# First product of an MLP's second stage made inside the last block of its first stage, and late weight differences queued behind factor splits

## The chip, the cores and the metric

The kernel runs on one core of one Trainium2 chip. A core has five engines with a queue of instructions each: TensorE (PE: matmuls, with PEld for its weight loads), VectorE (DVE), ScalarE (ACT), GpSimd (POOL) and SyncE (SP, which here only issues transfers). Each engine takes its instructions in the order that was fixed when the program was built; engines wait for one another through semaphores. The metric is the device time of one execution in microseconds; the figure of a kernel is the median over runs.

## The reference

One layer of a hybrid encoder: an input projection, a state-space mixer and a neighbourhood attention, an output projection, and an MLP. Only the last line matters here; the rest is left out. All arrays are float32, with 1024 tokens, `D_MODEL` = 1024 and `D_FF` = 4096.

```python
...
    x = x + jnp.concatenate([y_ssm, y_na.astype(y_ssm.dtype)], axis=-1) @ w_out
    h = rmsnorm(x, norm_mlp_w)
    return x + jnp.square(jax.nn.relu(h @ w_mlp_in)) @ w_mlp_out
```

## The kernel before

**Precision.** PE multiplies float32 operands that were rounded to a shorter form (`F32R`). So every operand is split: its high part is a copy by ACT into that form (line 761), its low part the rest, src - high, by DVE or POOL (line 762). `chain` (line 745) makes one matrix product of three matmuls: high x high, high x low, low x high. Weights are split with POOL for the low part, activations ("factors") with DVE.

**Both MLP stages** use a scheme of Strassen's kind: a product of two 2 x 2 block matrices takes seven block products instead of eight, in the order `ORD` = 1, 2, 6, 5, 7, 3, 4, over sums and differences of the blocks. Products 1, 6, 7 and 4 are summed in one set of PSUM banks (`X`), 2 in a second and 5 and 3 in a third (`Y`).

**Stage one** (lines 1124 to 1272) makes relu(h @ w_mlp_in)^2 in eight blocks of 512 columns (`Block`, fb = 0 to 7). A product is 24 matmuls of 128 x 128 by 512. Its factors `hc[1]` to `hc[7]` stay in SBUF for all blocks; the tiles of products 1 to 3 are tags `h10` to `h31` of pool `hA`. A block's weights come in four tiles ("11", "12", "21", "22", `raw_tile`, eight in a ring, two in pool `wp` and six in `wq`); `split` makes the high and low tile of a product's weights through `w_split` (line 1119), whose ring `hls` has three pairs `wh`/`wl`, all in `wp`. `X` is two of the four PSUM banks `mm` (`ps_mm`, line 107), so that two blocks' sums can be live at once. `sums` brings the results to SBUF, squares them, forms the factors of stage two, and `store` writes these to `act_dr`. In the last block the stores are issued by POOL, else by SP.

**Stage two** (lines 1275 to 1377) multiplies with `w_mlp_out` in four blocks of 1024 rows (fb = 0 to 3). A product is 48 matmuls: for each of four token tiles t, two halves u of the rows, two quarters a, and the three of `chain`. `a_load` reads a factor from `act_dr` (pool `ar`, four tiles), `a_split` splits it (`ahl`: pools `a1`, `a2`, `a3` with two pairs each), weights are loaded into `raw_of` tiles and split through `w_split`, now with `hls` = three pairs in `wy` and three in `wp`. Line 1373 adds each result to `acc`, which was loaded from `x2_dr` (line 1355). Before product 6 DVE forms the weight differences `t1` and `t2` (lines 1343 and 1344), before product 7 that of line 1346, before product 4 that of line 1348.

**Places.** Pools are placed over one another: the tiles of stage two lie where stage one's lay, and each waits for the last use of the tile below it. By sizes and sides, `ar` lies over `h10` and `h11`, `a1` over `h20` and `h21`, `a2` over `h30` and `h31`, `ra` (weights "21") and `x0` (the first half of `acc`) over the tiles of products 7 and 4, `rb` (weights "12" and "22") over the factors of 6 and 5, `wy` over `wq`, and `x1` and `a3` over the tiles `cq` of `sums`. PSUM pool `ps3` of stage one is closed at its end, and `ps4` takes its banks.

**Order.** Nobody writes out the queues. At build a scheduler runs the traced program through a model of the machine and puts next on each engine, among the instructions that are ready there, the one traced first. A tile of a pool with several buffers is given a buffer when one is free. `tc.issue_after(i)` keeps what is traced within it behind instruction i on the same engine, without a wait.

## Time and profile before

| what | value |
|---|---|
| median of 3 runs | 1672.34 us (1671.72 to 1681.54) |
| the profiled execution, its own time | 1682.42 us |
| its span in the trace | 1680.6 us |
| granted TensorE clock, mean | 0.984 |
| DVE, ACT, POOL busy in the span | 1031.1, 722.1, 727.7 us |
| HBM read, written | 189.40 MB, 86.56 MB |
| last block of stage one, from its product 1 | from about 1318.3 us of the span |
| stage two, from its first matmul | from 1361.15 us to the end |

The profile's views used here are: the page (busy time of each engine), rows of busy time by stretch (start and end in microseconds of the span, length, busy time and count for each engine, granted TensorE clock, share of the DMA engines and GB/s), rows of instructions in order of time (start, length, engine, line, operation, output<-inputs, shape, count, and in brackets the idle time of the engine before it with what ended it), and the chain of waits (start, length, engine, output, line). Names are those of the program without buffer numbers: `px`, `py`, `pz` are PSUM banks, `wh` and `wl` weights' high and low parts, `h` stage one's factors, `ahl` stage two's, `wraw` weights as loaded, `cq` stage one's results. A matmul's end is modelled and overlaps the next one's start. Line 747 is the matmul in `chain` for both stages: `px<-h,wh` is stage one, `px<-wh,ahl` stage two.

### The profile page before, as it was taken

The numbers are of one execution on the slowest core, as the hardware profiler recorded it, in microseconds if no ns is written. First come the engines' busy times: TensorE is split into PE (matmuls) and PEld (weight loads), VectorE is DVE, ScalarE is ACT, GpSimd is POOL, SyncE is SP. The second block draws the span as 40 slices with busy tenths as digits, with TensorE's granted clock in tenths as the row PEclk, the third lists the DMA queues.
The fourth block names the chain that finished last, engine by engine and source line by source line (L and its number), as shares of the span: only waits on it lengthen the run. The fifth ranks groups of instructions, "written<-read, shape, count | busy, mean of one in ns | idle before, by whom it ended". The sixth has DMA issues, their size and how long they took to land. (4 is left out here: it accounts for less than half of the span.)

```text
span 1680.6 us, 20886 instructions
## 1 busy us (share of the span) xinstructions
PE 1596.8 (95%) x7461; PEld 1301.1 (77%) x7461; DVE 1031.1 (61%) x1438; ACT 722.1 (43%) x1195; POOL 727.7 (43%) x522
## 2 busy tenths in 40 slices
PE   6999999999988889999999989999999979999999
PEld 5788888777776678887887867788888868888887
DVE  5776314788886853566675567444343387887863
ACT  5434223334343432566566533544444544433330
POOL 4000003877787861233335233344444464455551
PEclk9999999999999999999999999999999999999999
DMA  8213336866675885978565241353344386644231
GB/s 207 61 38 104 90 99 195 218 195 186 226 231 176 221 256 192 275 201 221 167 183 169 89 150 51 113 178 136 138 163 151 114 294 243 213 151 150 100 101 75
DMA packets 180290, 274.01 MB, mean 163 GB/s; under 512 B 14603, under 2 KB 105819, under 8 KB 180187
## 3 DMA queue, kind: packets, MB, share of 16 engines
q1 hardware_dynamic: 136203, 231.77, 45.1%
q10 hardware_dynamic: 42976, 37.23, 7.3%
q0 software_dynamic: 1008, 3.67, 0.5%
q8 instruction: 59, 0.97, 0.2%
q14 instruction: 44, 0.36, 0.1%
HBM read 189.40 MB, written 86.56 MB: 164 GB/s over the span
## 5 line engine op out<-in xcount | busy, mean ns | idle before, releaser
L762 POOL TENSOR_TENSOR wl<-wraw,wh 128x1024 fp32r<-128x1024 f32 x110 | 299.7, 2736 | 317.6 <-ACT wh L761 303.1
L761 ACT ACTIVATE wh<-wraw 128x1024 fp32r<-128x1024 f32 x110 | 115.6, 1054 | 151.2 <-PE px L747 51.2
L747 PE MATMUL px<-wh,ahl 128*128 128x512 f32 x512 | 160.8, 391 | 4.6 <-ACT ahl L761 3.3
L180 PE MATMUL pq<-wh,hTh 128*128 128x512 f32 x384 | 154.3, 404 | 5.7 <-ACT wh L150 5.6
L181 PE MATMUL pq<-wl,hTh 128*128 128x512 f32 x384 | 153.8, 402 | 3.8 <-DVE wl L151 3.8
L747 PE MATMUL px<-h,wh 128*128 128x512 f32 x496 | 156.0, 396 | 1.4 <-DVE x L1103 1.4
L182 PE MATMUL pq<-wh,hTl 128*128 128x512 f32 x384 | 153.4, 401 | 0.0
L762 DVE TENSOR_TENSOR ahl<-ar,ahl 128x1024 fp32r<-128x1024 f32 x56 | 115.1, 2062 | 22.9 <-ACT ahl L761 21.8
L761 ACT ACTIVATE ahl<-ar 128x1024 fp32r<-128x1024 f32 x56 | 58.2, 1052 | 140.0 <-PE px L747 74.7
L747 PEld LDWEIGHTS px<-wh,ahl 128*128 128x128 f32 x512 | 96.0, 188 | 25.9 <-ACT ahl L761 3.7
L747 PEld LDWEIGHTS px<-h,wh 128*128 128x128 f32 x496 | 93.2, 188 | 24.0 <-ACT h L186 1.6
L151 DVE TENSOR_TENSOR wl<-wraw,wh 128x1024 fp32r<-128x1024 f32 x40 | 54.0, 1355 | 82.3 <-ACT wh L150 81.7
L747 PE MATMUL px<-wl,ahl 128*128 128x512 f32 x256 | 99.8, 390 | 0.0
L747 PE MATMUL px<-h,wl 128*128 128x512 f32 x248 | 98.1, 396 | 0.0
L180 PEld LDWEIGHTS pq<-wh,hTh 128*128 128x128 f32 x384 | 74.1, 193 | 22.2 <-ACT wh L150 7.2
L181 PEld LDWEIGHTS pq<-wl,hTh 128*128 128x128 f32 x384 | 74.0, 193 | 20.9 <-DVE wl L151 6.2
L614 POOL TENSOR_TENSOR rb<-rb,c 128x512 f32<-128x512 f32 x64 | 76.6, 1218 | 21.8 <-DMA rb<-cum_dr 21.7
L182 PEld LDWEIGHTS pq<-wh,hTl 128*128 128x128 f32 x384 | 73.9, 192 | 15.2
L186 ACT ACTIVATE pth<-ptp 128x384 fp32r<-128x384 f32 (+1 forms) x128 | 56.8, 456 | 67.3 <-PE ptp L961 66.7
L747 PE MATMUL pz<-h,wh 128*128 128x512 f32 x256 | 82.0, 401 | 0.7 <-DVE h L187 0.7
L150 ACT ACTIVATE wh<-wraw 128x1024 fp32r<-128x1024 f32 x58 | 61.1, 1056 | 46.3 <-PE px L181 19.2
L747 PE MATMUL pz<-wh,ahl 128*128 128x512 f32 x256 | 80.5, 390 | 0.0
(271 smaller groups left out, 4087.5 us busy)
## 6 DMA issues: line engine op xcount, KB each, us to landing
ar<-act_dr SPq DMA_DIRECT2D x56, 512.0 KB, 3.7
act_dr<-cq SPq DMA_DIRECT2D x49, 512.0 KB, 3.2
wraw<-in_w_in_dram SPq DMA_DIRECT2D x44, 512.0 KB, 4.5
rb<-cum_dr SPq DMA_DIRECT2D x32, 512.0 KB, 7.1
wraw<-in_w_mlp_in_dram SPq DMA_DIRECT2D x32, 512.0 KB, 4.6
wraw<-in_w_mlp_out_dram SPq DMA_DIRECT2D x32, 512.0 KB, 5.5
q_dr<-hl ACTq DMA_DIRECT2D x64, 128.0 KB, 3.2
k_dr<-hl ACTq DMA_DIRECT2D x16, 512.0 KB, 5.3
```

Source lines behind the costliest of these rows:

```text
L150: nc.scalar.activation(hi[:, 0:n], raw[:, 0:n], AF.Copy)
L151: lo_eng.tensor_tensor(lo[:, 0:n], raw[:, 0:n], hi[:, 0:n].bitcast(F32), op=sub)
L180: nc.tensor.matmul(pt, lhsT=ah, rhs=bh, start=first, stop=False)
L181: nc.tensor.matmul(pt, lhsT=ah, rhs=bl, start=False, stop=False)
L182: return nc.tensor.matmul(pt, lhsT=al, rhs=bh, start=False, stop=last)
L186: nc.scalar.activation(hi, src, AF.Copy)
L614: nc.gpsimd.tensor_tensor(rb[:, d], rb[:, d], c1[:, d, c, h0 : h0 + 4].unsqueeze(2).broadcast_to([P, 4, P]), op=sub,)
L747: nc.tensor.matmul(pt, lhsT=a, rhs=b, start=f, stop=l, skip_group_check=True)
L761: nc.scalar.activation(hl[0], src, AF.Copy)
L762: eng.tensor_tensor(hl[1], src, hl[0].bitcast(F32), op=sub)
```

## The change

Behind product 6 of block 7 a new function `begin_out` is traced. It loads the two factor halves of stage two's product 1 of fb = 0 into one tile of tag `h10`, loads the two weight halves "11" into the two `wraw` tiles of `wp`, splits the factors into tiles of tags `h20` and `h21`, splits the weights through `w_split` with stage one's ring of three pairs, takes four `mm` banks and makes product 1 into them. Stage two takes over the loaded weights and the banks, and for product 1 only adds the banks to `acc`. To that end the PSUM pool `ps3` stays open for both stages, the rings of `raw_a` and `ahl` start at 2, and the matmul loop, the weight load and the factor load become functions.

Apart from that, the differences of lines 1346 and 1348 are put behind the factor split on DVE that was traced last.

```diff
     def split_to(hl, src, eng):
         nc.scalar.activation(hl[0], src, AF.Copy)
-        eng.tensor_tensor(hl[1], src, hl[0].bitcast(F32), op=sub)
+        return eng.tensor_tensor(hl[1], src, hl[0].bitcast(F32), op=sub)
...
+    phase["ps"] = ctx.enter_context(
+        tc.tile_pool(name="ps3", bufs=1, space=PSUM, reuse_waits="tile")
+    )
+    phase["mm"] = 4
+
+    def out_products(i, X, Y, wa, add_to):
+        for t in range(4):
+            pt = (X if i in (1, 6, 7, 4) else Y)[t]
+            for u in range(2):
+                (ah, al), (wh, wl) = wa[u]
+                for a in range(2):
+                    s = slice(a * 512 + t * P, a * 512 + t * P + P)
+                    d = slice(a * 512, a * 512 + 512)
+                    chain(
+                        pt, ah[:, s], al[:, s], wh[:, d], wl[:, d],
+                        i in (1, 2, 5) and u + a == 0, u + a == 2,
+                    )
+            if add_to is not None:
+                add_to(i, t, pt)
...
+        def begin_out():
+            ar = hA.tile([P, 2, 1024], F32, tag="h10", name="ar0")
+            raw, wa = [], []
+            for u in range(2):
+                out_factor(ar[:, u], 0, 1, u)
+                raw.append(wp.tile([P, 1024], F32, tag="wraw", name="wraw", bufs=2))
+                out_weights(raw[u], 0, u, "11")
+            for u in range(2):
+                t = hA.tile([P, 2, 1024], F32R, tag=f"h2{u}", name="ahl0")
+                hl = t[:, 0], t[:, 1]
+                split_to(hl, ar[:, u], nc.vector)
+                wa.append((hl, w_split(raw[u], nc.gpsimd)))
+            X = [ps_mm("px2") for _ in range(4)]
+            out_products(1, X, None, wa, None)
+            return raw, X
...
                 kb.sums(i)
+                if (fb, i) == (7, 6):
+                    begun_out = begin_out()
     b0s.close()
...
-        phase["ps"] = ph.enter_context(
-            tc.tile_pool(name="ps4", bufs=1, space=PSUM, reuse_waits="tile")
-        )
...
-        ring["rb"] = ring["ahl"] = 0
+        ring["rb"] = 0
+        ring["raw"] = ring["ahl"] = 2
...
         def a_split(ar):
             pool = ahl[ring["ahl"] % 6]
             ring["ahl"] += 1
             t = pool.tile([P, 2, 1024], F32R, tag="ahl", name="ahl", bufs=2)
-            split_to((t[:, 0], t[:, 1]), ar, nc.vector)
+            turn["split"] = split_to((t[:, 0], t[:, 1]), ar, nc.vector).ins
             return t[:, 0], t[:, 1]
+
+        turn = {}
+
+        def behind(key):
+            return tc.issue_after(turn[key]) if key in turn else nullcontext()
...
+            X = begun_out[1] if fb == 0 else [ps_mm("px2") for _ in range(4)]
...
                     elif i == 7:
-                        nc.vector.tensor_tensor(q["12"], q["22"], q["12"], op=sub)
+                        with behind("split"):
+                            nc.vector.tensor_tensor(q["12"], q["22"], q["12"], op=sub)
                     elif i == 4:
-                        nc.vector.tensor_tensor(q["21"], q["21"], q["t2"], op=sub)
+                        with behind("split"):
+                            nc.vector.tensor_tensor(q["21"], q["21"], q["t2"], op=sub)
+                    if (fb, i) == (0, 1):
+                        continue
...
+                if (fb, i) == (0, 1):
+                    for t in range(4):
+                        add_out(i, t, X[t])
+                else:
+                    out_products(i, X, Y, wa, add_out)
```

`out_weights` and `out_factor` hold the two transfers as they stood, and `add_out` the lines from 1370 to 1377.

## What the change should do to the time

> **What bounds the kernel now.** I read the page first, then busy time by stretch, then the PE rows at the seam between the two MLP stages, then the chain of waits.
>
> ```profile
> span 1680.6 us, 20886 instructions
> PE 1596.8 (95%) x7461; PEld 1301.1 (77%) x7461; DVE 1031.1 (61%) x1438; ACT 722.1 (43%) x1195; POOL 727.7 (43%) x522
> ```
>
> ```profile
> 1318.30:1357.80 39.50, 39.50 (x170) 31.55 (x168) 18.22 (x16) 17.59 (x22) 18.08 (x9) 1.00 0.62 226
> 1357.80:1381.20 23.40, 14.80 (x62) 11.22 (x61) 22.56 (x11) 12.97 (x14) 19.65 (x11) 0.98 0.74 270
> 1381.20:1392.10 10.90, 10.89 (x36) 8.67 (x37) 5.54 (x8) 1.18 (x2) 2.23 (x2) 0.73 0.88 326
> 1392.10:1676.90 284.80, 284.75 (x1249) 234.06 (x1247) 207.78 (x180) 96.13 (x98) 142.45 (x48) 1.00 0.43 144
> ```
>
> The first fence is from the page; the rows of the second (stretch, length, then busy PE, PEld, DVE, ACT, POOL, granted clock, DMA) are the seam by stretches. They show that PE is full in the last block of stage one, full again from 1392.1 to the end at clock 1.00, and short of work only between. So all that this change can win lies in that seam; in the rest of stage two it can only lose.
>
> ```profile
> 1357.47 0.39 PE L747 MATMUL px<-h,wl 128*128 128x512 f32 x1
> 1361.15 0.50 PE L747 MATMUL px<-wh,ahl 128*128 128x512 f32 x1 [3.29 <-ACT ahl L761]
> ...
> 1381.21 1.22 PE L747 MATMUL py<-wh,ahl 128*128 128x512 f32 x2 [3.81 <-DVE ahl L762]
> ...
> 1392.06 0.39 PE L747 MATMUL px<-wh,ahl 128*128 128x512 f32 x1
> ```
>
> ```profile
> 1363.36 3.47 DVE ahl L762 x2
> ...
> 1367.77 2.40 DVE wraw L1348
> ...
> 1371.10 3.43 DVE ahl L762
> 1374.53 3.35 DVE wraw L1348
> 1377.88 3.29 DVE ahl L762
> ...
> 1381.21 11.01 PE py L747 x35
> 1392.22 10.89 PE px L747 x48
> ```
>
> In the PE rows (start, length, and in brackets the idle time before and its releaser) the last matmul of stage one starts at 1357.47, product 6 of stage two at 1392.06. In between PE makes products 1 and 2. A product of 48 matmuls takes 10.89 at full clock (last row), so 2 x 10.89 = 21.78 of 1392.06 - 1357.47 - 0.23 (one matmul) = 34.36 is work, and **12.6 us is lost**: idle before 1361.15 and before 1381.21, some shorter gaps, and a half-speed stretch (35 matmuls in 11.01). The chain of waits says why: VectorE makes the low parts of the factors (ahl) one after another, with two weight differences of line 1348 (2.40 and 3.35) between them. 12.6 us is the ceiling of the gain, 0.75% of the median.
>
> **The change part by part.** Product 1 of stage two moves, with its two factor loads, two weight loads, two factor splits and two weight splits, to behind product 6 of block 7. No matmul, split or transfer is added or taken away; the terms are waits.
>
> *PSUM.* px2 needs four banks of a ring of four. Two were block 6's and are free. The other two are block 7's own sums X, which products 7 and 4 still add to. Their last readers:
>
> ```profile
> 1357.05 0.57 ACT L1215 ACTIVATE cq<-px 128x512 f32<-128x512 f32 x1
> ...
> 1358.47 0.59 ACT L1215 ACTIVATE cq<-px 128x512 f32<-128x512 f32 x1
> ```
>
> So only t = 0 and 1, 24 matmuls or 10.89 / 2 = 5.45 us, can run inside the block; t = 2 and 3 follow its product 4. The wait for the copies is 0 (t = 2 covers the second, t = 3's) to 1 us (a copy of 0.59 and its signal); I take 0.
>
> *Weight splits.* This is the term that decides. The moved splits no longer use the fresh tiles of wy but the stage-one ring hls, three pairs wh/wl. That ring is already exactly used up:
>
> ```profile
> 1318.53 1.06 ACT L761 ACTIVATE wh<-wraw 128x1024 fp32r<-128x1024 f32 x1 [2.02 <-PE px L747]
> ...
> 1324.86 1.06 ACT L761 ACTIVATE wh<-wraw 128x1024 fp32r<-128x1024 f32 x1
> ...
> 1329.71 1.06 ACT L761 ACTIVATE wh<-wraw 128x1024 fp32r<-128x1024 f32 x1 [3.32 <-issue]
> ...
> 1335.33 1.06 ACT L761 ACTIVATE wh<-wraw 128x1024 fp32r<-128x1024 f32 x1 [2.01 <-PE px L747]
> ...
> 1340.91 1.06 ACT L761 ACTIVATE wh<-wraw 128x1024 fp32r<-128x1024 f32 x1 [2.03 <-PE pz L747]
> ```
>
> ```profile
> 1335.30 0.63 PE L747 MATMUL pz<-h,wh 128*128 128x512 f32 x2
> 1335.76 0.40 PE L747 MATMUL pz<-h,wl 128*128 128x512 f32 x1
> ```
>
> ```profile
> 1336.47 2.39 POOL L762 TENSOR_TENSOR wl<-wraw,wh 128x1024 fp32r<-128x1024 f32 x1 [2.50 <-ACT wh L761]
> ...
> 1364.20 19.19 POOL L762 TENSOR_TENSOR wl<-wraw,wh 128x1024 fp32r<-128x1024 f32 x6
> ```
>
> The ACT copies are the splits for products 6, 5, 7, 3, 4. From 1324.86 on they stand about 5.6 us apart, one product's time, and each starts as a product ends: that for 3 at 1335.33, where product 6 ends and product 5's matmuls begin (1335.30). So a split gets its pair when the product three places earlier is done. Going back 5.6 us each, product 2 ended at 1329.7 and product 1 at 1324.1. In the new order the pairs go to 6, then to the two moved splits b0 (end of product 1) and b1 (end of product 2), then to 5 (end of product 6, 1335.3). The loop runs over t outside and u inside, so b0 and b1 are both held until t = 3, which is after product 4. Products 5, 7, 3 and 4 are left **one** pair, whichever it is (in strict turn 7 would wait for b0's, and b0 for a bank that product 7 fills): each split can start only when the product before it has ended. The first such wait, before product 5, is covered by the 5.45 us of t = 0 and 1 (1335.30 + 5.45 = 1340.75, where POOL's split below is done at 1338.86). The three before products 7, 3 and 4 have no cover.
>
> What one costs: PE needs wl at its third matmul, 0.46 behind the first (1335.30 to 1335.76). ACT starts at 1335.33 and POOL ends at 1336.47 + 2.39 = 1338.86, so 1338.86 - 1335.76 = 3.1 us. Where DVE works beside it, as from 1364.20, a POOL split takes 19.19 / 6 = 3.2, and the wait is 3.9. DVE makes the differences of stage two there, so I take 3.5: **3 x 3.5 = 10.5 us**, between 9.3 and 11.7.
>
> *The clock.* Each such wait can also lower the granted clock:
>
> ```profile
> 1357.90:1361.10 3.20, 0.00 (x0) 0.00 (x0) 2.46 (x3) 3.17 (x5) 0.97 (x2) 1.00 0.71 191
> ...
> 1380.20:1387.00 6.80, 5.79 (x14) 4.54 (x15) 4.72 (x7) 0.00 (x0) 3.19 (x1) 0.50 0.64 224
> ...
> 547.30:554.10 6.80, 5.90 (x14) 4.22 (x15) 4.95 (x10) 2.85 (x6) 6.64 (x7) 0.50 0.44 88
> ```
>
> ```profile
> 548.20 0.80 PE L589 MATMUL pcb<-cT,bT 128*128 128x128 f32 x2 [3.03 <-DVE st L552]
> ```
>
> An idle 3.2 us at 1357.9 left it at 1.00; the 3.03 before 548.20 went with 0.50 for 6.8 us, which costs 3.4, as the 3.81 did at 1380.2. So 0 to 3.4 for each of three waits, 0 to 10.2. I take 2.5, less than one fall in the three waits, because two matmuls run inside each wait once wh is there.
> The Trainium skill, "TensorE: Matmul & The Clock Gate", section "HAM oscillation — how this bites in real kernels", says that only idle gaps above some 3.4 us re-throttle; by that rule this term would be 0 and the sum lower by 2.5. The trace does not bear the threshold out: the 3.03 us gap went with half clock.
>
> *Factor splits and loads.*
>
> ```profile
> 1289.24 0.38 SPq L1326 DMA_DIRECT2D wraw<-in_w_mlp_out_dram  x1
> ...
> 1319.84 5.02 SPq L1204 DMA_DIRECT2D act_dr<-cq  x4
> 1335.49 0.38 SPq L1326 DMA_DIRECT2D wraw<-in_w_mlp_out_dram  x1
> ```
>
> The two factor loads wait for product 1 of block 7 (1324.1), whose tile h10 they take. The SyncE queue issues nothing from 1319.84 + 5.02 = 1324.9 to 1335.49, so they pass nothing and have 5.6 us to land before product 2 frees h20 and h21; the loads from 1335.49 on, which wait for products 6 and 5, keep their place behind them. The second of the two weight loads was issued at 1289.24 already, and both stay that early.
>
> ACT then has two factor copies and b1's copy of 1.06 beside the sums of product 2, and POOL b1's split of 2.39, so b1 is complete at 1329.7 + 3 x 1.06 + 2.39 = 1335.3 at the earliest order that puts it last, just as product 6 ends: 0 to 1 us of wait, I take 0.5. POOL's stores of block 7 stand behind these splits by up to 2.4 us; they are read back in the last block only, hundreds of us later, so 0.
>
> *Differences queued back.* Lines 1346 and 1348 go behind a factor split on DVE. At the seam that takes 2.40 + 3.35 from ahead of product 2's factors, part of the 12.6. Later the split of product 4 waits for its difference, but pairs come free two products ahead, 21.8 us, against 1.06 + 3.43 + 3.35 + 1.06 + 3.2 = 12.1 for a factor split, a difference and a weight split at the slow rows above: 0, where losing this cover would cost up to one 3.35 difference in each of three blocks.
>
> *Sum.* Product 2's two weight splits follow split 4 on POOL, 2 x 3.2 = 6.4 us, while PE makes product 4 and t = 2, 3 (5.6 + 5.45), and its factors need no more than a2, free after product 3: product 2 starts without a wait, so the 12.6 goes. In its place stand 10.5 + 2.5 + 0.5 + 0 = 13.5. Net 13.5 - 12.6 = +0.9. The profiled execution took 1682.42 with its span of 1680.6, 10.1 above the median of 1672.34, so such an execution would come out at 1683.3, and the median at **1673.2**.
>
> **The rivals.**
> *A: the pairs do not bind,* because the splits of 5, 7, 3 get theirs first or b0 and b1 let go sooner. For it: every split in the quoted rows was early. Against: b0's weights are in SBUF well before 1324.1, so it is ready when the pair comes free. Price: 12.6 less 0.5 to 2 is won, about 1661.
> *B: slower, by one copy at the wrong place in ACT's queue.* Engines keep the order fixed at build, and this one is already bad at one place:
>
> ```profile
> 1390.92 1.06 ACT L761 ACTIVATE wh<-wraw 128x1024 fp32r<-128x1024 f32 x1 [14.91 <-PE py L747]
> ```
>
> That copy stood 14.91 us at the head of ACT's queue for a pair, with a factor copy behind it. With the moved splits holding pairs to the seam's end, the same in front of the copy for product 3 or 4 stalls PE for that time: 1673.2 + 14.9 + 3.4 of clock = 1691.5. It decides over 1% only when the block is longer than about 16 us with its clock loss; here against it stands that ACT served every stage-one copy within a microsecond of its product.
> *C: the clock falls in all three waits* and POOL always takes 3.2: 11.7 + 10.2 + 1 + 1 - 12.6 = +11.3, or 1683.6.
>
> **How the numbers follow.** The forecast with its own range (9.3 - 12.6 = -3.3 to C's +11.3, 1669 to 1684) has 0.68, of which C, its upper end, 0.08; A has 0.22, B 0.07, and 0.03 is left for a seam where the first half also comes late. About 1%, 16.7 us, is what a measurement of this kernel can tell from no change. Faster by more than that needs a gain beyond the ceiling: 0.02. Slower by more is B and some of the rest: 0.08. Within 1%: 0.90. The range reaches from A to C: 1660 to 1684.
>
> **What would show it.** Right: a run of 24 px matmuls from ahl between products 6 and 5 of block 7, and 24 behind product 4; three gaps of about 2 to 4 us before products 7, 3 and 4, ended by POOL wl, each ACT copy starting as the product before ends; product 2 starting without a gap; no L1348 between two ahl rows. A is right if PE runs from 1335 to stage two's product 6 without gaps. B is right if ACT idles over 10 us with PE idle too. Wrong altogether: new gaps after product 6 of stage two.

## The result and the profile after

The changed kernel takes 1694.97 us (median of 4 runs, 1693.09 to 1700.11), the kernel before 1672.77 in the same comparison: a ratio of 1.0119 with a 95% interval of 1.0096 to 1.0142 (the quotient of the two medians is 1.0133), some 20 us slower. The prediction was 1673.2 with a range of 1660 to 1684; the time lies 11 us above its upper end.

To see where the time went I cut the end of the execution at places that every version has, read from the start times of the matmuls in the trace. T0 is the end of product 6 of block 7. The **seam** runs from T0 to the start of product 6 of stage two; its work on PE alone is 4 x 5.6 + 2 x 10.89 = 44.2 us. The **first block** runs from there to the start of product 2 in the next block (fb = 1); six products make 65.3 us of work. The **rest** runs to the end.

| | seam | first block | rest | from T0 |
|---|---|---|---|---|
| before | 56.8 | 65.7 | 222.9 | 345.3 |
| after | 64.8 | 76.0 | 224.1 | 364.9 |
| difference | +8.0 | +10.3 | +1.2 | +19.6 |

The seam lost 12.6 us before and loses 20.6 now; the first block, which ran without a gap, loses 10.7. (The profiled span itself went only from 1680.6 to 1691.3, because what lies ahead of T0 took 9 us less in this execution. Profiled executions of these kernels reach T0 at 1326 to 1335 us, with nothing changed there, so times are compared from T0 on.)

The stretches of the changed kernel (columns as in the prediction's stretch rows):

```profile
1326.40:1331.90 5.50, 5.50 (x25) 4.50 (x24) 0.23 (x1) 1.53 (x2) 3.17 (x2) 1.00 0.60 191
1331.90:1337.60 5.70, 5.70 (x25) 4.34 (x24) 0.08 (x1) 0.61 (x2) 0.00 (x0) 1.00 0.00 1
1337.60:1346.00 8.40, 6.18 (x25) 4.36 (x24) 3.84 (x4) 1.58 (x3) 2.36 (x1) 1.00 0.53 187
1346.00:1357.40 11.40, 8.93 (x25) 6.40 (x24) 2.69 (x5) 3.27 (x4) 3.15 (x2) 0.70 0.68 231
1357.40:1365.60 8.20, 6.00 (x25) 4.58 (x26) 4.51 (x4) 3.50 (x5) 4.01 (x4) 1.00 0.26 106
1365.60:1371.10 5.50, 5.50 (x25) 4.30 (x23) 1.97 (x1) 3.66 (x4) 3.49 (x4) 1.00 1.01 285
1371.10:1391.20 20.10, 13.99 (x49) 10.88 (x49) 12.96 (x11) 7.90 (x8) 13.65 (x5) 0.83 0.94 347
1391.20:1467.30 76.10, 68.49 (x290) 55.05 (x289) 59.96 (x47) 26.99 (x28) 36.77 (x12) 0.98 0.53 187
```

They are, in order: t = 0 and 1 of product 1; block 7's products 5, 7, 3 and 4; t = 2 and 3; product 2; the first block. Products 7, 3 and 4 take 8.4, 11.4 and 8.2 us where 5.6 is work, together 11.2 too much. Product 2 takes 20.1 where 10.89 is work, 9.2 too much. That is 20.4 of the seam's 20.6. Every PE row of that time with idle time before it (in brackets the idle time and what ended it):

```profile
1338.68 1.19 PE L747 MATMUL px<-h,wh 128*128 128x512 f32 x4 [0.97 <-ACT wh L761]
1341.12 0.50 PE L747 MATMUL px<-h,wl 128*128 128x512 f32 x1 [1.25 <-POOL wl L762]
1347.03 1.20 PE L747 MATMUL pz<-h,wh 128*128 128x512 f32 x4 [0.97 <-ACT wh L761]
1349.68 0.79 PE L747 MATMUL pz<-h,wl 128*128 128x512 f32 x1 [1.46 <-POOL wl L762]
1358.33 1.19 PE L747 MATMUL px<-h,wh 128*128 128x512 f32 x4 [0.98 <-ACT wh L761]
1360.80 0.50 PE L747 MATMUL px<-h,wl 128*128 128x512 f32 x1 [1.27 <-POOL wl L762]
1376.18 0.77 PE L747 MATMUL py<-wh,ahl 128*128 128x512 f32 x1 [4.93 <-ACT ahl L761]
1378.12 0.80 PE L747 MATMUL py<-wl,ahl 128*128 128x512 f32 x1 [1.18 <-POOL wl L762]
1404.64 0.49 PE L747 MATMUL pz<-wh,ahl 128*128 128x512 f32 x1 [2.14 <-ACT ahl L761]
1407.25 0.73 PE L747 MATMUL pz<-wh,ahl 128*128 128x512 f32 x2 [0.49 <-DVE ahl L762]
1454.65 0.68 PE L747 MATMUL px<-wh,ahl 128*128 128x512 f32 x1 [4.98 <-DVE acc L1365]
```

The first six rows are the three forecast waits: each time a gap for wh, a few matmuls, and a gap for wl. The next two, before and in product 2, and the last three, in the first block, were not forecast; "new gaps after product 6 of stage two" was the prediction's own sign of being wrong altogether. The ACT rows and the SyncE rows behind these:

```profile
1369.90 1.06 ACT L761 ACTIVATE wh<-wraw 128x1024 fp32r<-128x1024 f32 x1 [1.67 <-PE px L747]
1371.28 3.90 ACT L761 ACTIVATE wh<-wraw 128x1024 fp32r<-128x1024 f32 x4 [0.32 <-PE px L747]
1375.08 1.99 ACT L761 ACTIVATE ahl<-ar 128x1024 fp32r<-128x1024 f32 x2
...
1402.59 1.06 ACT L761 ACTIVATE wh<-wraw 128x1024 fp32r<-128x1024 f32 x1 [21.11 <-PE px L747]
1403.55 3.88 ACT L761 ACTIVATE ahl<-ar 128x1024 fp32r<-128x1024 f32 x4
```

```profile
1381.42 3.86 SPq L1147 DMA_DIRECT2D wraw<-in_w_mlp_out_dram  x6
1385.89 25.06 SPq L1153 DMA_DIRECT2D ar<-act_dr  x7
```

Two things stand out as suspects. ACT has weight copies that wait for PE, one of them 21.11 us, ahead of factor copies. And SyncE issues six weight tiles of the next block (3 MB) ahead of the factor loads for products 5, 7 and 3 of this one.

### The profile page after: what moved, and what is told of

Same layout as the page of the kernel before. It is cut to its first block, busy times and chain, and to the rows that moved or that the text cites. A ratio compares the mean times of both kernels' runs of the same rounds, so it can differ in the third digit from the quotient of the medians.

```text
span 1691.3 us, 20888 instructions
## 1 busy us (share of the span) xinstructions
PE 1599.2 (95%) x7461; PEld 1299.2 (77%) x7461; DVE 1041.1 (62%) x1438; ACT 722.7 (43%) x1195; POOL 721.4 (43%) x522
## 4 chain that ended last, share of the span: by engine, by line
PE 64%; DMA 10%; DVE 9%; POOL 7%; issue 7%; ACT 2%; SPq 1%; ACTq 0%; DVEq 0%; POOLq 0%
PE px L747 19%; PE pz L747 9%; PE py L747 5%; PE po L180 3%; PE po L182 3%; PE po L181 3%; PE px L180 3%; PE px L181 3%; PE px L182 3%; DMA rb<-cum_dr 2%; PE pv L909 2%; POOL rb L614 2%; PE pz L181 2%; PE pz L180 2%; PE pz L182 2%
## 5 line engine op out<-in xcount | busy, mean ns | idle before, releaser
L762 POOL TENSOR_TENSOR wl<-wraw,wh 128x1024 fp32r<-128x1024 f32 x110 | 292.6, 2669 | 349.5 <-ACT wh L761 340.8
L151 DVE TENSOR_TENSOR wl<-wraw,wh 128x1024 fp32r<-128x1024 f32 x40 | 54.4, 1363 | 81.4 <-ACT wh L150 80.8
L186 ACT ACTIVATE pth<-ptp 128x384 fp32r<-128x384 f32 (+1 forms) x128 | 56.8, 456 | 67.4 <-PE ptp L961 66.8
L150 ACT ACTIVATE wh<-wraw 128x1024 fp32r<-128x1024 f32 x58 | 61.0, 1056 | 50.2 <-PE px L181 18.7
```

The lines of the kernel that those rows point to most:

```text
L150: nc.scalar.activation(hi[:, 0:n], raw[:, 0:n], AF.Copy)
L151: lo_eng.tensor_tensor(lo[:, 0:n], raw[:, 0:n], hi[:, 0:n].bitcast(F32), op=sub)
L186: nc.scalar.activation(hi, src, AF.Copy)
L762: return eng.tensor_tensor(hl[1], src, hl[0].bitcast(F32), op=sub)
```

## The experiments

All changes are to the changed kernel unless said otherwise. Letters of the theories as the expectations use them: P, the held pairs make the loss; Q, the differences queued back make it; R, the waits come from POOL's or ACT's order and not from pairs; S, copies at the head of ScalarE's (ACT's) queue; T, the order or rate of transfers; U, the work of VectorE (DVE) as such; V, other tiles that product 1 takes early. In edited kernels lines shift by up to 6: L763 and L764 are lines 761 and 762, L1149 and L1155 the two loads of lines 1147 and 1153.

| kernel | seam | first block | rest | ratio to before, 95% interval |
|---|---|---|---|---|
| 1 no queue-back | 72.4 | 70.0 | 224.1 | 1.0142 (1.0125 to 1.0159) |
| 2 before, queue-back only | 50.2 | 72.7 | 222.9 | 1.0008 (0.9996 to 1.0021) |
| 3 one pair held | 56.5 | 73.9 | 224.1 | 1.0059 (1.0036 to 1.0081) |
| 4 one pair held, no queue-back | 59.4 | 71.8 | 224.1 | 1.0084 (1.0061 to 1.0107) |
| 5 ACT in order | 66.0 | 73.6 | 224.1 | 1.0120 (1.0087 to 1.0152) |
| 6 only factors early | 63.3 | 65.7 | 222.9 | 1.0044 (1.0029 to 1.0060) |
| 7 as 6, ACT in order | 58.6 | 65.7 | 222.9 | 1.0012 (0.9997 to 1.0028) |
| 8 as 2, ACT in order | 48.8 | 73.3 | 222.9 | 0.9998 (0.9982 to 1.0014) |
| 9 as 6, acc loads later | 51.1 | 74.2 | 222.9 | 1.0022 (1.0007 to 1.0037) |
| 10 as 9, ACT in order | 46.3 | 76.2 | 222.9 | 0.9997 (0.9979 to 1.0015) |
| 11 as 10, next weights later | 46.3 | 65.7 | 222.9 | 0.9943 (0.9923 to 0.9962) |
| 12 half of product 1 moved | 59.2 | 74.7 | 222.9 | 1.0072 (1.0049 to 1.0095) |
| 13 as 12, next weights later, ACT in order | 54.4 | 65.7 | 222.9 | 0.9997 (0.9986 to 1.0009) |
| 14 next weights later | 66.5 | 66.0 | 224.1 | 1.0048 (1.0031 to 1.0065) |
| 15 as 14, ACT in order | 61.8 | 66.0 | 224.1 | 1.0068 (1.0050 to 1.0086) |
| 16 as 2, next weights later | 47.4 | 65.7 | 222.9 | 0.9954 (0.9937 to 0.9972) |

The stages are of one profiled execution each, the ratios of all runs.

### 1 and 2: are the differences queued back to blame?

```diff
-                        with behind("split"):
-                            nc.vector.tensor_tensor(q["12"], q["22"], q["12"], op=sub)
+                        nc.vector.tensor_tensor(q["12"], q["22"], q["12"], op=sub)
```

and the same for product 4 (run 1); the kernel before with only these two differences queued back (run 2).

> The change without its second part: the differences before products 7 and 4 are free to go ahead again. Stretches: seam = end of block 7's product 6 to product 6 of stage two's first block (56.8 us before, 64.8 with the change); first block = from there to product 2 of the second block (65.7 and 76.0); rest (222.9 and 224.1). Theory P (the moved product holds two of three weight pairs to the seam's end; everything else follows from it): seam 63 to 67 with the three waits before products 7, 3 and 4; first block still 72 to 78, since weight copies that wait for pairs stand ahead of the factor copies on ACT; in all about +18 us, ratio 1.010 to 1.014. Rival Q (the differences queued back cost the 10 us of the first block): seam 63 to 67, first block 65 to 68, in all about +8 us, ratio 1.004 to 1.007.

> The kernel before with only the second part of the change: differences behind factor splits, no moved product. Theory P: the two differences leave the chain ahead of product 2's factors, so the seam falls from 56.8 us to 50 to 55, the first block stays at 65 to 68; ratio 0.996 to 1.001. Rival Q: the first block rises by 6 to 12 us to 72 to 78; ratio 1.002 to 1.007.

Q falls for the time as a whole: without the queue-back the changed kernel is at 1.0142, with it at 1.0119, and alone it leaves the kernel before as it was, 1.0008. But the stages show that "no difference" is a balance. In run 2 the seam is 6.6 us shorter than before and the first block 7.0 longer; run 1 against the changed kernel shows the same from the other side, a seam 7.6 longer and a first block 6.0 shorter. Its 70.0 us in the first block lie between what P (72 to 78) and Q (65 to 68) expected, and its seam of 72.4 above what either did. So the queue-back does cost the first block 6 to 7 us. Run 16 shows by what way for the kernel before.

### 3 and 4: one pair less

```diff
-                wa.append((hl, w_split(raw[u], nc.gpsimd)))
+                if u == 0:
+                    wt = hA.tile([P, 2, 1024], F32R, tag="h11", name="whl0")
+                    whl = wt[:, 0], wt[:, 1]
+                    split_to(whl, raw[u], nc.gpsimd)
+                else:
+                    whl = w_split(raw[u], nc.gpsimd)
+                wa.append((hl, whl))
```

The first moved weight split gets a tile of its own (tag `h11`), so that products 5, 7, 3 and 4 have two pairs. Run 4 is without the queue-back.

> The change, but the first of the two moved weight splits goes into the tile h11, which product 1 of block 7 has used up, so that only one of the three pairs is held and each later split can start two products ahead of its own. Theory P: the three PE waits before products 7, 3 and 4 vanish (none above 0.5 us), block 7's end comes 8 to 11 us sooner, seam 50 to 57 us; in the first block 66 to 76; ratio 0.995 to 1.006. Rival R (the waits come from POOL or ACT order, not from the pairs): the three waits stay at 2 us or more each, seam 62 to 67, ratio 1.010 to 1.014.

> The same with h11 and without the second part of the change. Theory P: as with h11, seam 50 to 57, first block 66 to 76, within 4 us of the run with h11. Rival Q: the first block is 6 us or more shorter than with h11 and the differences queued back, at 65 to 68; ratio 0.992 to 0.999.

Run 3's PE rows with idle time before them, from T0 (1331.85) through product 2:

```profile
1370.40 0.80 PE L747 MATMUL py<-wh,ahl 128*128 128x512 f32 x1 [4.93 <-ACT ahl L761]
1371.81 0.80 PE L747 MATMUL py<-wl,ahl 128*128 128x512 f32 x1 [0.61 <-POOL wl L762]
1377.53 0.73 PE L747 MATMUL py<-wh,ahl 128*128 128x512 f32 x2 [2.48 <-DVE ahl L762]
```

The three waits before products 7, 3 and 4 are gone with the one pair, so they come from the pairs and R falls for them. From T0 to the end the time falls from 364.9 to 354.5. Run 4 takes 355.2 us from T0, within 4 us of run 3 as P expected; its first block of 71.8 is not the 65 to 68 of Q. Product 2's wait and most of the first block's loss stay in both; they have other causes.

### 5: ScalarE in the order of the products

```diff
-                    wa.append((a_split(ar), w_split(src, nc.gpsimd)))
+                    with tc.issue_after(last_act) if fb == 0 and last_act is not None else nullcontext():
+                        wa.append((a_split(ar), w_split(src, nc.gpsimd)))
+                    if u == 1:
+                        last_act = acts[-2]
```

`acts` lists ACT's copies as they are traced, so `last_act` is the second factor copy of the product before.

> The changed kernel, with one thing more: in the first block of stage two, ScalarE takes each product's copies (weights and factors) behind the factor copies of the product before it. Marks: the seam (end of block 7's product 6 to the start of stage two's product 6) was 56.8 us before and 64.8 after; the first block (from there to the start of the next block's product 2) 65.7 and 76.0. Theory S (what is left of the loss beside the three waits comes from copies that wait for a pair at the head of ScalarE's queue): the 4.93 + 1.18 us of waits before product 2 and its half clock, 9.3 us, shrink to 2 or less, the 2.14 us wait before product 5 of the first block goes; the three waits of 2.2 to 2.8 us before products 7, 3 and 4 of block 7 stay. Seam 55 to 58, first block 66 to 72, ratio to the kernel before 0.999 to 1.006. Rival T (the loads at the seam are late, since transfers run at 334 GB/s there, and the queue only follows): the wait before product 2 stays over 4 us, now ended by a transfer; seam 62 or more, ratio 1.010 or more. Rival U (VectorE's work is the bound up to the end of the first block): seam and first block together stay at 140.8 within 2 us, whatever the seam wins.

The copies moved as meant, and nothing was won (1.0120). The wait only changed its place. Run 5's DVE row for the first of product 2's two factor splits, its POOL row beside it, and its PE row:

```profile
1373.73 9.65 DVE L764 TENSOR_TENSOR ahl<-ar,ahl 128x1024 fp32r<-128x1024 f32 x1 [1.62 <-ACT ahl L763]
```

```profile
1372.96 9.33 POOL L764 TENSOR_TENSOR wl<-wraw,wh 128x1024 fp32r<-128x1024 f32 x4
```

```profile
1383.44 1.22 PE L747 MATMUL py<-wh,ahl 128*128 128x512 f32 x2 [6.16 <-DVE ahl L764]
```

PE now starts product 2 with a gap of 0.5 us and stops in its middle for 6.16, because the first factor split on DVE takes 9.65 us beside four weight splits on POOL, and the second comes behind it. S falls as the whole cause of either loss: the first block took 73.6, still 8 too much. U's mark was met, seam and first block together being 139.6 against the 140.8 of the changed kernel; run 11 decides on U.

### 6 to 8: only the factors early

Run 6 keeps the early loads and the early factor splits of product 1 and leaves its weight splits and its matmuls in stage two:

```diff
-                wa.append((hl, w_split(raw[u], nc.gpsimd)))
-            X = [ps_mm("px2") for _ in range(4)]
-            out_products(1, X, None, wa, None)
-            return raw, X
+                wa.append(hl)
+            return raw, wa
...
                     if (fb, i) == (0, 1):
+                        wa.append((begun_out[1][u], w_split(q["11"], nc.gpsimd)))
                         continue
...
```

Run 7 adds ScalarE's order to it, run 8 adds that order to run 2.

> The changed kernel without moving the product: behind product 6 of block 7 only the loads of product 1 and the two splits of its factors are made; its weight splits and its 48 matmuls stay in stage two, with stage two's own pairs. No pair of stage one's ring is held. Theory P (pairs): the three waits before products 7, 3 and 4 (11.2 us) are gone, product 1 starts within 1 us of block 7's product 4. Theory S: the queue of ScalarE still has product 5's weight copies ahead of product 2's factors, but now they get their pairs earlier, so the wait before product 2 is 0 to 5 us. Seam 46 to 54, ratio 0.992 to 1.001. Rival R (the waits do not come from pairs): they stay at 2 to 3 us each, ratio 1.004 or more. Rival U: seam and first block together no shorter than the 122.5 of before, ratio 1.000 or more, however short the seam.

> The last one with ScalarE's copies of the first block of stage two in the order of its products. Theory S: product 2 starts with 1 us of wait or less; seam 44.2 (the work alone) to 48, first block 66 to 71, ratio 0.990 to 0.997, faster than the kernel before and than the one with only the factors early. Rival T: a wait of 2 us or more before product 2 or 6, ended by a transfer. Rival U: seam and first block together 121 or more, so that the first block takes 73 or more, ratio 0.998 or more.

> The kernel before with the differences queued back (no work moved) and ScalarE's copies of stage two's first block in the order of its products. Without that order it had a seam of 50.2 us and a first block of 72.7, 122.9 together against 122.5 before, ratio 1.001. Theory S: the order alone takes 3 to 7 us from the first block, ratio 0.996 to 0.999. Rival U: together 122 to 124 again, ratio 0.999 to 1.002, the wait of 3.6 us in the first block still ended by VectorE.

In run 6 no wait is left from T0 to the end of product 1, and then product 2 waits 16 us. This was expected by no theory; the SyncE rows show it (here L1411 is the load of `acc`):

```profile
1332.28 7.01 SPq L1147 DMA_DIRECT2D wraw<-in_w_mlp_out_dram  x4
1363.10 1.76 SPq L1411 DMA_DIRECT2D acc<-x_dr  x4
1364.96 1.80 SPq L1147 DMA_DIRECT2D wraw<-in_w_mlp_out_dram  x3
1366.81 1.74 SPq L1153 DMA_DIRECT2D ar<-act_dr  x2
```

From 1339.3 to 1363.1 SyncE issued nothing: at the head of its queue stood the second half of `acc`, which lies over `cq` and waits for block 7's last stores, and product 2's weights and factors stood behind it. The first block is full (65.7), with the seam long. In run 7 product 2 still waits 12.58 us, far from the 1 us or less of S: its weight copies wait 17.62 us for a transfer, with the same loads of `acc` ahead of it in SyncE's queue, so T's mark is met. Run 8 changed nothing that can be measured against run 2; seam and first block together are 122.1 us, as U expected.

### 9 to 11: two more orders in SyncE's queue

Run 9 puts the loads of `acc` behind product 2's loads in run 6. Run 10 adds ScalarE's order. Run 11 adds one thing more to run 10, the next block's first weight loads behind product 7's factor loads:

```diff
-                    for t in range(4):
-                        begun = nc.sync.dma_start(acc[h][:, t, :], x2_dr[4 * h + t])
+                    with tc.issue_after(acc_behind):
+                        for t in range(4):
+                            begun = nc.sync.dma_start(acc[h][:, t, :], x2_dr[4 * h + t])
...
-                    order.enter_context(tc.issue_after(begun.ins))
+                    order.enter_context(tc.issue_after(next_behind))
...
+                if (fb, i) == (0, 7):
+                    next_behind = turn["load"]
```

(`turn["load"]` is the last factor load traced, `acc_behind` that of product 2.)

> Factors early, product in its place, and the eight loads of acc (which stood ahead of product 2's loads in SyncE's queue and waited there for block 7's last stores, 23.8 us in the run without this) put behind product 2's loads. Theory S (heads of queues): the 16 us wait before product 2 shrinks to 0 to 5; seam 46 to 53; first block 66 to 74; ratio 0.993 to 1.000. Rival U (a bound of VectorE, GpSimd and the transfers together that gives seam and first block at least the 122 us that the kernel before, the one with only the differences queued back, and the one with ScalarE in order all have): together 121 to 124, ratio 0.999 to 1.002.

> The last one with ScalarE's copies of the first block of stage two in the order of the products. Theory S: product 2 starts with 0 to 2 us of wait, seam 44 to 49, first block 66 to 73, together 110 to 120, ratio 0.991 to 0.998. Rival U: together 121 to 124, ratio 0.999 to 1.002, the first block losing what the seam wins in a wait for VectorE near its end.

> The last one, with the first loads of the next block's weights put behind the factor loads of product 7, so that the factors of products 5 and 7 do not stand behind 3 MB of weights that are needed 65 us later. If the transfers at the seam are what holds the first block (rival T), the factor splits of products 5 and 7 start 4 to 8 us earlier and seam and first block together are 3 to 8 us shorter than without this; if VectorE's own work is the bound (rival U), they are the same within 1.5 us.

Run 9 brought product 2's wait from 16 to 4.99 us and the seam to 51.1, as S expected, but the first block to 74.2 and the ratio to no better than 1.0022. Run 10 came out as U expected: the seam won 4.8 us more, the first block lost 2.0, together 122.5, ratio 0.9997. Run 11 tells U from T.

Runs 10 and 11 have the same seam, 46.3 us, 2.1 above its work, and first blocks of 76.2 and 65.7 us: **10.5 us from the order of SyncE's queue alone**. First run 10's SyncE rows and the ACT row of product 5's first factor copy, then run 11's (run 10's seam ends at 1373.25, run 11's at 1373.28, so the times can be compared as they stand):

```profile
1368.07 1.59 SPq L1149 DMA_DIRECT2D wraw<-in_w_mlp_out_dram  x3
1369.76 0.58 SPq L1155 DMA_DIRECT2D ar<-act_dr  x1
1370.43 0.58 SPq L1149 DMA_DIRECT2D wraw<-in_w_mlp_out_dram  x1
1371.15 3.77 SPq L1155 DMA_DIRECT2D ar<-act_dr  x3
```

```profile
1382.38 1.06 ACT L763 ACTIVATE ahl<-ar 128x1024 fp32r<-128x1024 f32 x1 [13.97 <-DMA ar<-act_dr]
```

```profile
1368.16 6.61 SPq L1155 DMA_DIRECT2D ar<-act_dr  x4
1374.82 3.77 SPq L1149 DMA_DIRECT2D wraw<-in_w_mlp_out_dram  x6
```

```profile
1375.99 1.06 ACT L763 ACTIVATE ahl<-ar 128x1024 fp32r<-128x1024 f32 x1 [7.53 <-DMA ar<-act_dr]
```

Product 5's factors arrive 6.4 us earlier. What that does at the other end, 55 us later, is read from two stretches, of run 10 and of run 11:

```profile
1373.25:1428.00 54.75, 54.75 (x241) 44.88 (x239) 48.12 (x34) 23.10 (x24) 32.38 (x11) 1.00 0.66 233
1428.00:1436.50 8.50, 0.09 (x2) 0.04 (x1) 8.50 (x8) 2.82 (x3) 4.70 (x2) 0.63 0.48 176
```

```profile
1373.28:1428.00 54.72, 54.72 (x242) 45.11 (x241) 49.51 (x42) 23.52 (x24) 30.56 (x11) 1.00 0.72 261
1428.00:1436.50 8.50, 8.50 (x39) 6.92 (x38) 6.24 (x7) 2.73 (x3) 6.24 (x2) 1.00 0.53 182
```

In run 10 PE runs full for 54.75 us and then stands for 8.4, with DVE busy all the time: DVE could not start its splits early, fell behind, and the additions to `acc` that free a PSUM bank came late. In run 11 DVE did 1.4 us more in the first stretch, 42 instructions instead of 34, and PE never stops. U falls: seam and first block together are 112 us here, though five kernels without a held pair (the one before and runs 2, 7, 8 and 10) had given 122 to 124. That sum looked like a bound, and was two queue orders.

Run 11 has the lowest time of all, 1664.58 us (1663.69 to 1665.72), 0.9943 of the kernel before. Only its interval and that of run 16 lie below 1.

### 12 and 13: half of product 1 moved, no pair held

```diff
...
-            out_products(1, X, None, wa, None)
-            return raw, X
+            out_products(1, X, None, wa, None, range(2))
+            return raw, X, wa
...
                     if (fb, i) == (0, 1):
+                        wa.append((begun_out[2][u][0], w_split(q["11"], nc.gpsimd)))
                         continue
...
                 if (fb, i) == (0, 1):
+                    out_products(i, X, Y, wa, None, range(2, 4))
```

(The last argument of `out_products` is the range of t.) Only t = 0 and 1 are made in block 7; for t = 2 and 3 the weights are split again. Run 13 adds two orders, ScalarE's and that of the next block's weights; the order of the `acc` loads, which run 11 has too, it does not have.

> The changed kernel, in which only the first half of product 1 (token tiles t = 0 and 1) is made within block 7, so that the two pairs of stage one's ring come free again right behind product 6's end plus 5.5 us; for t = 2 and 3 the two weight splits are made a second time, with stage two's pairs (two ACT copies and two POOL splits more, 6.9 us of work off PE). Theory P (the pairs that are held to the end of the block make the loss, the three waits directly and the rest through the splits of products 2, 6 and 5 that pile up behind them): the three waits before products 7, 3 and 4 (11.2 us) are gone, product 2 waits 5 us or less; seam 46 to 54, seam and first block together 118 to 126 as in the kernel before (122.5), against 140.8; ratio 0.996 to 1.003. Rival V (not the pairs but the placement of the other tiles, that is, factors and loads that product 1 takes early, costs what the three waits do not explain, 7 us or more): seam and first block together 127 or more, ratio 1.004 or more.

> Half of product 1 within block 7, its weights split a second time for the other half (so no pair is held beyond product 6), with the two orders (ScalarE's copies, next block's weights later). Against factors early and product in place with the same two orders (seam 46.3, first block 65.7, ratio 0.994) this tells what the moved product itself brings: by the sum of work on PE nothing, since there PE waits only 1.7 us in all. Seam 45 to 50, first block 65.3 to 67, ratio 0.993 to 0.998. If the two repeated weight splits pile up on GpSimd beside VectorE's factor splits, product 2 has a wait of 3 to 6 us in its middle and the seam is 50 to 56.

In run 12 the three waits are gone, as P says, and the seam still takes 59.2: product 2 waits 5.27 and 4.43 us. So product 2's wait needs no held pair. Seam and first block together are 133.8 us and the ratio is 1.0072, so the marks of V were met and the rest of P's were not; but V's reason, the factors and loads that product 1 takes early, falls with run 11, which takes the same ones early and has 112.0. Run 13 beside run 11 shows what makes the wait, since in neither a pair is held from products 7, 3 and 4, and they differ in where half of product 1 stands. By their edits they differ in two things more, and neither shows in the traces here: SyncE's loads around product 2 stand in the same order in both (four of `acc`, then two factors, from 1349.57 us in run 11 and from 1355.46 in run 13), and POOL makes four splits beside product 2's first factor split in both (9.46 and 9.32 us). ACT rows of the last copy of block 7's sums and of product 2's copies, run 11 (T0 at 1326.98):

```profile
1350.21 1.06 ACT L1255 ACTIVATE cq<-cq 128x1024 f32<-128x1024 f32 x1
1351.18 1.99 ACT L763 ACTIVATE wh<-wraw 128x1024 fp32r<-128x1024 f32 x2
1353.07 1.99 ACT L763 ACTIVATE ahl<-ar 128x1024 fp32r<-128x1024 f32 x2
```

and run 13 (T0 at 1327.37):

```profile
1356.10 1.06 ACT L1255 ACTIVATE cq<-cq 128x1024 f32<-128x1024 f32 x1
1357.07 1.99 ACT L763 ACTIVATE wh<-wraw 128x1024 fp32r<-128x1024 f32 x2
1358.96 1.99 ACT L763 ACTIVATE ahl<-ar 128x1024 fp32r<-128x1024 f32 x2
```

Product 2's copies stand behind the last copies of block 7's sums, which come as block 7 ends. Half of product 1 inside the block makes the block end some 5.5 us later, so product 2's preparation starts 29.7 us behind T0 instead of 24.2. It takes as long in both (the first DVE split stands for 9.77 and 9.65 us beside POOL). In run 11 the 10.89 us of product 1 cover it and 1.7 us of waiting are left; in run 13 only the second half of product 1, 5.45 us, is left as cover, and PE waits 0.62 and 6.10 us and has half clock for 6.8. The moved half costs 54.4 - 46.3 = 8.1 us. The seam and the wait in product 2's middle are the second outcome that run 13's expectation names; the splits on POOL that it gives as the reason stand in run 11 too, without such a wait. Why the copies were put behind the last sums at build, and whether they could stand earlier, no run here shows.

### 14 and 15: the changed kernel with these orders

Run 14 has only the next block's weights later, run 15 ScalarE's order too.

> The changed kernel, with only this more: the first loads of the next block's weights stand behind the factor loads of product 7 in SyncE's queue, so that the factors of product 5 do not wait behind six weight tiles (3 MB). Theory T (the 10.3 us that the first block of stage two lost come from that order of transfers): the first block goes from 76.0 to 65.3 to 69, the wait of 4.98 us for VectorE near its end is gone; the seam stays 63 to 67; ratio to the kernel before 1.004 to 1.008 (it was 1.012). Theory S (ScalarE's copies, of which one waited 21.1 us for a pair ahead of product 5's factor copies): the first block stays at 72 or more. Rival U (VectorE's work): seam and first block together stay at 138 or more.

> The last one with ScalarE's copies of the first block in the order of the products too. If order T and order S are both needed for the first block, it is 65.3 to 67 here and 68 to 74 in the last one; if T alone does it, both are 65.3 to 67. The seam: the three waits (11 us) stay, and product 2's wait moves into its middle (6 us and the clock) as in the run with ScalarE's order alone: 63 to 67. Ratio 1.004 to 1.007. If the held pairs cost no more than the three waits, the seam is 57 or less.

The first block goes from 76.0 to 66.0 in both, the ratio from 1.0119 to 1.0048: T is right for the first block. In run 14 the scheduler also put the copy with the 21.11 us wait behind product 5's factor copies, of itself; that move alone was run 5, and gave 73.6. ScalarE's order on top brings nothing measurable (the intervals of 14 and 15 overlap; run 15's seam of 61.8 was profiled in an execution without a clock fall at the three waits). The seam stays long in both, as pairs and moved work say.

### 16: the kernel before, queue-back and next weights later

> The kernel before with the differences queued back (no work moved) and the next block's weights behind product 7's factor loads. Without the latter: seam 50.2, first block 72.7, ratio 1.001. Theory T: the first block goes to 65.3 to 67 and the seam stays 49 to 52: ratio 0.994 to 0.998, so that the differences queued back win their 6.6 us once the transfers let them. Rival U: together 121 to 124 as in five kernels without a held pair, ratio 0.999 to 1.002.

The first block is full and the seam 47.4, ratio 0.9954: once the loads allow it, the differences queued back do win what they cost DVE at the seam. It moves no work at all. Its interval and that of run 11 overlap, so the early factors of run 11 have no shown value of their own. The order of the loads without the queue-back was not run on the kernel before; that kernel had no gap in its first block, but the seam of run 16 is 2.8 us shorter than that of run 2, so what each of the two wins at the seam is not told apart.

## Why the prediction was wrong

Right were these steps. *PSUM* and *factor splits and loads*: t = 0, 1 and t = 2, 3 run without a wait. *Weight splits*: pairs decide, the wait before product 5 is covered, and the three before products 7, 3 and 4 are there, each ACT copy starting as the product before ends; run 3 shows that one pair more takes them away. Their size: 10.5 + 2.5 of clock was forecast, 7.8 + 3.4 = 11.2 came. Two things made the first part smaller: DVE was idle beside most of POOL's splits, which took 2.4 us and not 3.2, and four matmuls, not two, ran in each wait before wl was needed. That the sum of the two came so near is partly luck, since the clock term was too low.

Three steps failed.

*"Product 2 starts without a wait, so the 12.6 goes."* 9.2 us of waits stand before and in product 2. The step counted POOL's splits and the place of the factors, and put product 2's splits under product 4 and t = 2, 3. But ACT's first weight copy behind that for product 4 starts at 1365.59, as block 7 ends, and the factor copies of product 2 at 1375.08, behind four weight copies; and t = 0, 1 and the three waits push the end of block 7 back. What was taken for a gain, 24 matmuls made early, was cover for product 2. Run 13 has that cost without held pairs, 8.1 us. The ceiling of 12.6 was not reached through moved matmuls by any run; it was nearly reached (46.3 and 47.4 against 44.2 of work) where no matmul was moved.

*The sum ended at the seam.* It was said that "in the rest of stage two it can only lose", and then only the differences queued back were priced there. SyncE's queue was followed up to 1335.49 and no further. In the new program the next block's six weight tiles stand ahead of product 5's factor loads, and the first block lost 10.3 us. Run 11 takes 10.5 us back by that order alone; run 14 takes back 10.0 with that edit, which also moved a copy on ACT. The term that was priced there, the differences queued back, was put at 0 because pairs come free early, which says nothing of transfers: the kernel before, without a loss in that block, lost 7.0 us there with the queue-back alone, and run 16 takes these back by the order of the loads.

*Rival B* named the right kind, a queue with one instruction at the wrong place, and a price (18.3 us) near the whole loss, but put it in ACT's queue, in front of products 3 and 4 of block 7, and gave it 0.07; that the price came near is luck. Such a copy was found, 21.11 us at the head of ACT's queue in the first block; taking it away (run 5) brought 2.4 us in that block and nothing in the time. The range failed because it held rivals for the seam only.

The account of the 19.6 us from T0: 11.2 for the three waits, 9.2 for product 2, 10.3 for the first block, 1.2 for the rest, less the 12.6 lost before, 19.3 in all. The 1.2 us of the rest, 0.4 in a block, appear in every kernel whose whole product 1 was moved and in no other; their cause stays open.

## What to carry to other kernels

Work moved ahead to a place where PE is already busy wins nothing there, makes everything that hangs on the end of that stretch start later, and is missing where it covered something; ask what it covered before asking whether its operands are free. When a change shifts which tiles are free when, a scheduler may order every queue anew: follow the transfer queue through at least one whole block behind the change, and look for large loads for later ahead of small loads for now. A sum that stays the same over several versions (122 us here) can still be an order and not a bound.

## What was unexpected of the hardware

**One DVE split outlasted four POOL splits.** In the kernel before, POOL's six splits took 3.2 us each on average and DVE's operations beside them 3.4, in turns. In runs 5, 11 and 13 POOL made four in 9.3 to 9.5 us, 2.3 to 2.4 each, as fast as with nothing beside it, and one DVE split that takes 1.2 us elsewhere stood for 9.65 to 9.77; in run 5 it ended 1.1 us after POOL's fourth (1372.96 + 9.33 = 1382.29; 1373.73 + 9.65 = 1383.38). The Trainium skill, "SBUF — State Buffer", section "SBUF: two separate sides", says that the two engines share a pair of ports as an exclusive lock, that a DVE instruction with two inputs in SBUF, as this split has, and a POOL instruction that reads SBUF contend for it, and that the one that starts first has the pair for its whole instruction while the other stands still. The trace agrees for POOL's first split, which started 0.77 us ahead in run 5 (1372.96 and 1373.73); why POOL's second, third and fourth split went ahead of a DVE split that already waited, and why the two took turns in the kernel before, no run here shows.

**The same waits with and without a clock fall.** Each of the three forecast waits is two gaps of 1.0 and 1.2 to 2.0 us with four matmuls between them. All three stand in each of five kernels (the changed one and runs 1, 5, 14 and 15). Stretches around them in run 14 and in run 15:

```profile
1341.00:1344.40 3.40, 3.05 (x7) 2.47 (x8) 0.98 (x1) 0.00 (x0) 0.30 (x1) 0.51 0.86 333
1351.20:1354.60 3.40, 3.40 (x9) 2.63 (x10) 0.00 (x0) 0.00 (x0) 0.33 (x1) 0.50 0.92 252
1361.40:1364.80 3.40, 3.40 (x10) 2.61 (x9) 2.97 (x3) 0.00 (x0) 1.21 (x3) 0.51 0.38 154
```

```profile
1343.00:1347.00 4.00, 2.60 (x10) 1.86 (x11) 0.22 (x1) 0.58 (x2) 2.35 (x1) 1.00 0.87 292
1351.00:1356.00 5.00, 3.17 (x12) 2.28 (x13) 1.34 (x2) 2.56 (x3) 3.03 (x2) 1.00 0.77 246
1360.00:1366.00 6.00, 4.73 (x19) 3.54 (x20) 3.84 (x3) 2.49 (x3) 3.45 (x3) 1.00 0.22 87
```

All three went with half clock in run 14 (3.4 us each, which costs 1.7), as in runs 1 and 5, none in run 15, one in the changed kernel's profile (6.9 us at 0.51). In run 14 the half-clock stretches begin 10.2 us apart. The Trainium skill, "TensorE: Matmul & The Clock Gate", section "HAM oscillation — how this bites in real kernels", gives the rule as "no PE-idle gaps >~3.4µs"; these gaps are all shorter, and ten of the fifteen waits went with a fall, so the trace does not bear that threshold out.
